# Reading each projection out of PSUM once, with second buffers for keys and queries in the first layer

## The chip, the cores and the metric

The kernel runs on one core of one Trainium2 chip. The metric is the device time of one execution in microseconds (us). The profile is one execution, taken by the hardware profiler on that core. Its engines: TensorE (PE: matrix products and transposes, with its weight loads as PEld), VectorE (DVE), ScalarE (ACT), GpSimd (POOL) and SyncE (SP), whose queue starts most of the DMAs. Matrix products end in PSUM, which has eight banks; one bank holds 128 x 512 floats. Everything else lies in SBUF.

## The reference

One step of a two-layer encoder in float32, with 16 query heads and 4 key/value heads of width 64 and a model width of 1024. There are 1024 tokens of a new stream (8 tiles of 128) and 8 x 16 tokens of running streams with caches (a ninth tile, ST).

```python
# layer 0
qkv = rmsnorm(x, g_norm) @ w_qkv
q = rmsnorm(q.reshape(b, t, N_HEADS, HEAD_DIM), g_q)
k = rmsnorm(k.reshape(b, t, N_KV_HEADS, HEAD_DIM), g_k)
s = q @ k.T * HEAD_DIM ** -0.5 + bias         # own chunk of 64 + 2 before, with sinks
h = h + softmax(s) @ v @ w_o
h = h + square(relu(rmsnorm(h, g) @ w_up)) @ w_down
# layer 1: keys and values by w_kv, queries by w_q_b, own chunk + 8 before,
# learned bias by distance, no sinks; then the same kind of MLP
```

The change lies in what happens between a projection and the normed key or query: each head of 64 values is divided by the root of its mean square.

## The kernel before

**Precision and products.** Each operand is split into a high and a low part (`split`, L106: a copy cast to fp32r, then a subtraction), and each product is made of three matmuls: high by high, high by low, low by high. So a projection of one tile of 128 tokens to 512 columns is 8 x 3 = 24 matmuls of 128 x 512 (`proj`, L182; lines L186 to L188). The MLP has a scheme of its own that saves matmuls; it is not touched.

**Stages.** Per layer: attention, the rest of the output projection with the turning of the residual rows (`wo_phase`), MLP up, MLP down. By the lines at work in the trace, layer 0 runs attention to about 395 us, the handover to the MLP to about 460, up to about 812, down to about 1142. Layer 1 runs attention to about 1640, the handover to about 1690, up to about 2045, down to the end.

**Attention.** For each tile `K1` projects to keys and values (512 columns, 256 each) and `Q1` to queries of half the heads (512 columns). `Q1` runs over all tiles for the first half of the heads and later over all tiles again for the second half; the second time the split hidden rows (tiles hh, hl) come back from DRAM (`R`). When a projection is done, its stage-1 function empties the PSUM bank:

- `kv_stage1` (L237): V is written twice by L245 (ScalarE) and L246 (VectorE), in some tiles once more by L251; the raw keys are copied to kr (L252, ScalarE) and their squares go to kn (L253, ScalarE). kr and kn are the two halves of one tile, kw. Then reduction (L255), scaled mean (L257), power -1/2 on GpSimd (L259), product (L260) and the product with the gain into the tile ks (`k_stack`, L271).
- `q_stage1` (L190): squares to the scratch tile qn (L195, ScalarE), raw queries to the tile qr (L196, ScalarE), then reduction (L198), scaled mean (L203 or L205), power (L207, GpSimd) and product in place (L208).

Later `K2` and `Q2` turn ks and qr on TensorE (`transpose_pairs`, L229) and split the result into KT and qT. Then follow the scores (L349, L400 or L468), their exponentials, the transposes of the probabilities (L293), the products with V (L300, L301) and, half a layer later, the output projection (`WO`, L1474, with matmuls L147 to L149). A `WO` item of kind 0 puts its split input in tiles with the tags ks and kw, kind 1 two of the tag qr, kind 2 hh and hl.

**Buffers.** Tiles of one tag share a fixed number of buffers. A new tile waits until all users of the buffer's last tile are done. In layer 0, kw, ks and qr have one buffer each (2 KB per partition); in layer 1, qr has two. The PSUM role m, which most projections use, has one bank; role s has two in layer 0 and three in layer 1; all else in attention shares the remaining ones (role g).

**Order.** The source gives a program order (for instance three `K1` chunks woven together at the start, then `Q1` and `K2` in turn, then the `plan` of CFG). A planner at compile time turns that into one fixed list for each engine, by priorities and modelled durations (`schedule_with_timeline_sim=True`). On the chip an engine works through its list in order. Any change of buffers or dependencies can therefore also change the lists.

Of the kernel before, what the change touches and what calls it, by code (L numbers as in the profile page):

```python
# [8 lines left out]
F32 = mybir.dt.float32  # L9
F32R = mybir.dt.float32r  # L10
AF = mybir.ActivationFunctionType
# [5 lines left out]
P = 128  # L17
# [6 lines left out]
KV = 4  # L24
G = 4
HD = 64
# [49 lines left out]
class Build:  # L76
# [113 lines left out]
    def q_stage1(self, work, small, ps, t, nb, fold):  # L190
        nc = self.nc
        ps3 = ps.rearrange("p (h d) -> p h d", d=HD)
        qn = self.scratch([P, 8, HD], F32, "qn")
        qr = work.tile([P, 8, HD], F32, tag="qr", name="qr", bufs=self.qrb)
        nc.scalar.activation(qn, ps3, AF.Square)  # L195
        nc.scalar.copy(qr, ps3)  # L196
        ssq = small.tile([P, 8], F32, tag="qssq", name="qssq")
        nc.vector.tensor_reduce(ssq, qn, AX.X, ALU.add)  # L198
        ms = small.tile([P, 8], F32, tag="qms", name="qms")
        e = self.ex[:, t : t + 1]  # L200
        if fold:
            c = C_SL2 + nb * 8
            nc.vector.scalar_tensor_tensor(ms, ssq, e, self.cst[:, c : c + 8], ALU.add, ALU.mult)  # L203
        else:
            nc.vector.tensor_scalar(ms, ssq, e, 1.0 / HD, ALU.add, ALU.mult)  # L205
        rs = small.tile([P, 8], F32, tag="qrs", name="qrs")
        nc.gpsimd.tensor_tensor(rs, ms, self.mhalf[:, 0:8], ALU.pow)  # L207
        self.eng("q").tensor_tensor(qr, qr, rs.unsqueeze(2).to_broadcast([P, 8, HD]), ALU.mult)  # L208
        return qr
# [27 lines left out]
    def kv_stage1(self, work, small, ps, t, gk, gq8, gkq8, vst, v8, kout, vout):  # L237
        nc = self.nc
        ps3 = ps[:, 0:256].rearrange("p (h d) -> p h d", d=HD)
        kw = work.tile([P, 2, KV, HD], F32, tag="kw", name="kw")  # L240
        kr, kn = kw[:, 0], kw[:, 1]
        r = self.rx[:, t : t + 1]
        if vst is not None:
            pv3 = ps[:, 256:512].rearrange("p (h d) -> p h d", d=HD)
            nc.scalar.activation(vst[:, :, 0:HD], pv3, AF.Copy, scale=r)  # L245
            nc.vector.scalar_tensor_tensor(  # L246
                vst[:, :, HD:P], pv3, r, vst[:, :, 0:HD].bitcast(F32), ALU.mult, ALU.subtract
            )
        if vout is not None:
            vsb = v8 if v8 is not None else self.scratch([P, 256], F32, "vsb")  # L250
            nc.scalar.activation(vsb, ps[:, 256:512], AF.Copy, scale=r)  # L251
        nc.scalar.copy(kr, ps3)  # L252
        nc.scalar.activation(kn, ps3, AF.Square)  # L253
        ssq = small.tile([P, KV], F32, tag="kssq", name="kssq")
        nc.vector.tensor_reduce(ssq, kn, AX.X, ALU.add)  # L255
        ms = small.tile([P, KV], F32, tag="kms", name="kms")
        nc.vector.tensor_scalar(ms, ssq, self.ex[:, t : t + 1], 1.0 / HD, ALU.add, ALU.mult)  # L257
        rs = small.tile([P, KV], F32, tag="krs", name="krs")
        nc.gpsimd.tensor_tensor(rs, ms, self.mhalf[:, 0:KV], ALU.pow)  # L259
        nc.vector.tensor_tensor(kn, kr, rs.unsqueeze(2).to_broadcast([P, KV, HD]), ALU.mult)  # L260
        if kout is not None:
            nc.vector.tensor_tensor(kn, kn, gk.unsqueeze(1).to_broadcast([P, KV, HD]), ALU.mult)
            nc.sync.dma_start(kout, kn.rearrange("p h d -> p (h d)"))
        if vout is not None:
            nc.sync.dma_start(vout, vsb)
        return self.k_stack(work, kn, gq8 if kout is not None else gkq8)

    def k_stack(self, work, kn, gq8):
        nc = self.nc
        ks = work.tile([P, KV, HD], F32, tag="ks", name="ks")  # L270
        nc.vector.tensor_tensor(ks, kn, gq8.unsqueeze(1).to_broadcast([P, KV, HD]), ALU.mult)  # L271
        return ks

# [988 lines left out]
    def attention(self, layer):  # L1262
        nc, I = self.nc, self.ins
        A = layer == 0
# [12 lines left out]
        cfg = CFG[layer]  # L1277
        psp = () if A else cfg["psp"]
        self.engs = cfg["eng"]
        with ExitStack() as st:  # L1280
# [6 lines left out]
            work = self.pool(st, f"work{layer}")  # L1287
# [4 lines left out]
            up = self.pool(st, f"unit{layer}")  # L1292
# [6 lines left out]
            if cfg["rx"]:  # L1299
                self.raws += [(ring, "raw2")]  # L1300
            self.qrb = cfg["qrb"]
            self.KT = kvp.tile([P, NT, KV, 2, P], F32R, tag="KT", name="KT")
            self.VS = kvp.tile([P, NT, KV, P], F32R, tag="VS", name="VS")
            v8 = kvp.tile([P, 256], F32, tag="v8", name="v8")
# [169 lines left out]
            def WO(t, half):  # L1474
                o = self.scratch([P, 4, P], F32, "o")
                self.load_halves(layer, half, t, o, second)
                kind = cfg["wt"][t] if half else 0
                if kind == 0:
                    oh = work.tile([P, 4, P], F32R, tag="ks", name="oh")
                    ol = work.tile([P, 4, P], F32R, tag="kw", name="ol")  # L1480
                elif kind == 1:
                    oh = work.tile([P, 4, P], F32R, tag="qr", name="oh", bufs=self.qrb)
                    ol = work.tile([P, 4, P], F32R, tag="qr", name="ol", bufs=self.qrb)
                else:
                    oh = hpool.tile([P, 4, P], F32R, tag="hh", name="oh")
                    ol = hpool.tile([P, 4, P], F32R, tag="hl", name="ol")
                self.split(oh, ol, o, "pool" if "O" in self.engs else "act", "pool" if "o" in self.engs else "dve")
                home = cfg["xt"].get(("AB"[half], t))
                if home == "x":
                    xt = work.tile([P, D], F32, tag="x", name="xo", bufs=2)  # L1490
                elif home in ("hh", "hl"):
                    xt = hpool.tile([P, D], F32, tag=home, name="xo")
                else:
                    xt = self.rawp.tile([P, D], F32, tag="raw", name="xo")
                if home == "keep":
                    self.kept[t] = xt
                nc.sync.dma_start(xt, self.xd[t] if half else x_src(t))
                z = [oh, ol, xt, None]

                def chunk(i):  # L1500
                    n, k = i // 4, i % 4
                    if k == 0:
                        z[3] = self.psum(cfg["wr"][2 * half + n], [P, 512], "ps_mm")
                    ps = z[3]
                    nn = slice(n * 512, n * 512 + 512)
                    self.wo_proj(ps, oh, ol, wo[half], nn, [k])
                    if k == 3:
                        nc.vector.tensor_tensor(xt[:, nn], ps, xt[:, nn], ALU.add)
                        if n == 1:
                            (nc.gpsimd if half else nc.sync).dma_start(self.xd[t], xt)  # L1510

                return [lambda i=i: chunk(i) for i in range(8)]
# [7 lines left out]
            prio = st.enter_context(ExitStack())  # L1520
# [5 lines left out]
            if A:  # L1526
                g = self.load_gains(apool)
# [182 lines left out]
def make_plan(tail):  # L1710
    plan = {}
    for s in range(2 * NT):
# [35 lines left out]

CFG = [
    dict(banks=dict(g=(5, 1), s=(2, 1), m=(1, 1)), q_bufs=4, order={}, plan=make_plan({15: [('A', 0)], 17: [('A', 1)], 19: [('A', 2)], 21: [('A', 3)], 23: [('A', 4)], 25: [('A', 5)], 30: [('A', 6)], 31: [('A', 7)], 32: [('A', 8), ('B', 0), ('B', 4), ('B', 3)]}),  # L1750
        la=3, prio=0, xt={('A', 8): 'x', ('B', 3): 'x', ('B', 0): 'keep', ('B', 4): 'keep'}, late=0, eng='cgu', k2=3, q2=9, lead=3, sf=0, up=(99, 2, 0, 3), ld=((10, 10, 11, 11), (11, 12, 13, 14), (27, 28, 29, 30)), n='g', q='g', qrb=1, np=3, bias_bufs=3, p_bufs=3, psp=(), wr='mmmm', wt=(0, 0, 2, 0, 2, 2, 0, 1, 2), rx=1, kd=1, o2=0, sb=0),
    dict(banks=dict(g=(4, 1), s=(3, 1), m=(1, 1)), q_bufs=4, order={}, plan=make_plan({15: [('A', 0)], 17: [('A', 1)], 19: [('A', 2)], 21: [('A', 3)], 23: [('A', 4)], 25: [('A', 5)], 27: [('A', 8)], 28: [('A', 7)], 29: [('A', 6)], 31: [('B', 0), ('B', 4), ('B', 1)], 32: [('B', 5), ('B', 2), ('B', 3)]}),
        la=2, prio=1000, xt={('B', 0): 'keep', ('B', 4): 'keep', ('B', 1): 'hh', ('B', 5): 'hl', ('B', 2): 'hh', ('B', 3): 'hl'}, late=0, eng='Ogu', k2=3, q2=6, lead=9, sf=0, up=(4, 2, 0, 99), ld=((11, 11, 11, 11), (11, 11, 11, 11), (26, 27, 28, 29)), n='g', q='g', qrb=2, np=2, bias_bufs=2, p_bufs=10, psp=(), wr='mmmm', wt=(0, 0, 0, 1, 1, 1, 1, 1, 2), rx=0, kd=1, o2=1, sb=3),
]

TC_KW = dict(schedule_with_timeline_sim=True)
# [42 lines left out]
```

## Time and profile before

| | |
|---|---|
| median of 3 runs | 2405.27 us (2404.04 to 2407.24) |
| span of the profiled execution | 2399.3 us |
| TensorE busy | 2320.4 us |
| VectorE busy | 1626.3 us |
| ScalarE busy | 1217.9 us |
| mean granted TensorE clock | 0.992 |

The profile gives the span from the first to the last instruction; the execution's own time was not kept, so it is taken as the span and what lies around it: the median is 6.0 us above the span. A row of the timeline is start, length, engine, line, operation, output <- input, shapes, count, and in brackets the engine's idle time just before and what ended it. A row of the waits is who waited for whom: total us, times, longest.

### The profile page before, as it was taken

To read this page: it belongs to the slowest core of one execution; us is meant where nothing else is said; L and a number is where in the kernel's file an instruction comes from. 1 tells how busy PE (TensorE), PEld (TensorE's weight loads), DVE (VectorE), ACT (ScalarE), POOL (GpSimd) and SP (SyncE) were. 2 spreads that over 40 slices of the span, in tenths; PEclk is the share of its full clock that TensorE was granted. 3 is DMA by queue.
4 is the path that set the end of the run, shared out by engine and by line. 5 is a ranking of instruction groups with operands and counts; after the bars stand their busy time and mean duration, and the time that the engine had idled before them with its cause. 6 is when DMAs were issued, how large, how long until landed. Compare 5 with 4: busy or idle time off the path is not lost.

```text
span 2399.3 us, 33421 instructions
## 1 busy us (share of the span) xinstructions
PE 2320.4 (97%) x11621; PEld 1935.5 (81%) x11621; DVE 1626.3 (68%) x3002; ACT 1217.9 (51%) x2423; POOL 535.6 (22%) x828
## 2 busy tenths in 40 slices
PE   7998999899999999999999999998999999999999
PEld 6786877788888888888777788887888888888887
DVE  6687786755655777776567877877655555776674
ACT  4676675555555433232267666665655555333321
POOL 3343332312112100000333434344211211000000
PEclk9998999999999999999999999999999999999999
DMA  7345546244433874342743555555434435744332
GB/s 244 122 127 168 171 156 200 95 155 158 145 128 141 323 245 146 117 141 99 237 149 111 188 161 173 173 169 174 138 127 145 154 137 200 278 140 158 112 116 114
DMA packets 218457, 385.88 MB, mean 161 GB/s; under 512 B 50408, under 2 KB 125104, under 8 KB 211120
## 3 DMA queue, kind: packets, MB, share of 16 engines
q1 hardware_dynamic: 195136, 307.16, 39.0%
q0 software_dynamic: 21776, 71.84, 7.7%
q10 hardware_dynamic: 1376, 4.74, 0.5%
q8 instruction: 92, 1.51, 0.3%
q14 instruction: 77, 0.63, 0.1%
HBM read 246.47 MB, written 136.14 MB: 159 GB/s over the span
## 4 chain that ended last, share of the span: by engine, by line
PE 82%; DMA 7%; DVE 5%; ACT 2%; issue 2%; POOL 1%; SPq 1%; ACTq 0%; DVEq 0%; POOLq 0%
PE ps_x L715 9%; PE ps_x L717 9%; PE ps_x L716 9%; PE ps_y L717 7%; PE ps_y L716 7%; PE ps_y L715 7%; PE ps_mm L186 3%; PE ps_mm L188 3%; PE ps_mm L187 3%; PE ps_tr L293 2%; PE ps_mm L147 2%; PE ps_mm L149 2%; PE ps_mm L148 2%; PE ps_s L717 1%; PE ps_s L716 1%
## 5 line engine op out<-in xcount | busy, mean ns | idle before, releaser
L109 ACT CAST w<-r 128x2048 fp32r<-128x2048 f32 x56 | 107.1, 1913 | 322.9 <-PE ps_y L717 212.1
L715 PE MATMUL ps_x<-w,s 128*128 128x512 f32 x512 | 199.5, 390 | 2.7 <-DVE hc L854 2.1
L717 PE MATMUL ps_x<-w,s 128*128 128x512 f32 x512 | 199.4, 389 | 0.0
L716 PE MATMUL ps_x<-w,s 128*128 128x512 f32 x512 | 199.2, 389 | 0.0
L186 PE MATMUL ps_mm<-w,hh 128*128 128x512 f32 x432 | 175.0, 407 | 13.8 <-ACT kw L253 5.1
L188 PE MATMUL ps_mm<-w,hl 128*128 128x512 f32 x432 | 174.3, 403 | 1.7 <-DMA hl<-hTd 1.4
L187 PE MATMUL ps_mm<-w,hh 128*128 128x512 f32 x432 | 172.5, 400 | 0.7 <-DVE w L159 0.7
L109 ACT CAST s<-s 128x2048 fp32r<-128x2048 f32 x56 | 107.1, 1913 | 117.9 <-DMA s<-hd 108.6
L115 DVE TENSOR_TENSOR w<-r,w 128x2048 fp32r<-128x2048 f32 x56 | 128.2, 2290 | 51.9 <-ACT w L109 51.9
L715 PE MATMUL ps_x<-sx,w 128*128 128x512 f32 (+1 forms) x408 | 157.8, 387 | 4.6 <-ACT hc L834 2.7
L1021 DVE TENSOR_TENSOR x<-ps_y,x 128x512 f32<-128x512 f32 x136 | 92.3, 687 | 101.1 <-PE ps_y L717 101.0
L717 PE MATMUL ps_x<-sx,w 128*128 128x512 f32 (+1 forms) x408 | 154.1, 378 | 0.0
L716 PE MATMUL ps_x<-sx,w 128*128 128x512 f32 (+1 forms) x408 | 154.1, 378 | 0.0
L109 ACT CAST w<-ru 128x512 fp32r<-128x512 f32 (+1 forms) x160 | 110.0, 708 | 85.3 <-PE ps_y L716 32.0
L717 PE MATMUL ps_y<-w,s 128*128 128x512 f32 x384 | 149.5, 389 | 0.0
L716 PE MATMUL ps_y<-w,s 128*128 128x512 f32 x384 | 149.4, 389 | 0.0
L715 PE MATMUL ps_y<-w,s 128*128 128x512 f32 x384 | 149.4, 389 | 0.0
L115 DVE TENSOR_TENSOR s<-s 128x2048 fp32r<-128x2048 f32 x56 | 128.1, 2287 | 26.5 <-ACT s L109 26.5
L115 DVE TENSOR_TENSOR ptl<-ps_tr,pth 128x512 fp32r<-128x512 f32 x180 | 122.6, 685 | 24.8 <-ACT pth L109 19.0
L115 DVE TENSOR_TENSOR w<-ru,w 128x512 fp32r<-128x512 f32 (+1 forms) x160 | 126.6, 793 | 10.9 <-ACT w L109 10.8
L109 ACT CAST pth<-ps_tr 128x512 fp32r<-128x512 f32 x180 | 104.8, 594 | 47.9 <-PE ps_tr L293 39.3
L115 DVE TENSOR_TENSOR wq<-ru,wq 128x1024 fp32r<-128x1024 f32 x32 | 39.7, 1240 | 131.9 <-ACT wq L109 131.9
(280 smaller groups left out, 6573.3 us busy)
## 6 DMA issues: line engine op xcount, KB each, us to landing
s<-hd SPq DMA_DIRECT2D x56, 1024.0 KB, 4.7
ru<-in_w_up SPq DMA_DIRECT2D x64, 512.0 KB, 3.9
r<-in_w_down SPq DMA_DIRECT2D x32, 1024.0 KB, 5.7
hd<-hc POOLq DMA_DIRECT2D x128, 256.0 KB, 2.7
hd<-hs POOLq DMA_DIRECT2D x96, 256.0 KB, 2.5
x<-xd SPq DMA_DIRECT2D x41, 512.0 KB, 4.6
o<-oTd SPq DMA_DIRECT2D x52, 256.0 KB, 4.1
hTd<-hh SPq DMA_DIRECT2D x36, 256.0 KB, 4.5
```

The costliest lines, as they stand in the source:

```text
L109: a = nc.scalar.copy(hi, src)
L115: return a, e.tensor_tensor(lo, src, hi.bitcast(F32), ALU.subtract)
L147: nc.tensor.matmul(ps, oh[:, k, :], w[:, 0, k, nn], start=(k == 0), stop=False)
L148: nc.tensor.matmul(ps, oh[:, k, :], w[:, 1, k, nn], start=False, stop=False)
L149: nc.tensor.matmul(ps, ol[:, k, :], w[:, 0, k, nn], start=False, stop=(k == 3))
L186: nc.tensor.matmul(ps, a, w[:, 0, k, :], start=(k == 0), stop=False)
L187: nc.tensor.matmul(ps, a, w[:, 1, k, :], start=False, stop=False)
L188: nc.tensor.matmul(ps, b, w[:, 0, k, :], start=False, stop=(k == KC - 1))
L715: a = mm(ps, ah, bh, start=first, stop=False, skip_group_check=True)
L716: mm(ps, ah, bl, start=False, stop=False, skip_group_check=True)
L717: return a, mm(ps, al, bh, start=False, stop=last, skip_group_check=True)
L1021: tt(xs[t][:, N[n]], ps, xs[t][:, N[n]], ALU.add)
```

## The change

In both stage-1 functions the raw projection is copied out of PSUM first, and the square then reads the copy in SBUF. The tags kw and ks get a number of buffers from the configuration (`krb`), 2 in layer 0 and 1 in layer 1; `WO` names the same number for its kind 0. In the first entry of CFG `qrb` goes from 1 to 2; in the second it stays at 2. Nothing else in CFG changes.

```diff
         qn = self.scratch([P, 8, HD], F32, "qn")
         qr = work.tile([P, 8, HD], F32, tag="qr", name="qr", bufs=self.qrb)
-        nc.scalar.activation(qn, ps3, AF.Square)
         nc.scalar.copy(qr, ps3)
+        nc.scalar.activation(qn, qr, AF.Square)
...
-        kw = work.tile([P, 2, KV, HD], F32, tag="kw", name="kw")
+        kw = work.tile([P, 2, KV, HD], F32, tag="kw", name="kw", bufs=self.krb)
...
         nc.scalar.copy(kr, ps3)
-        nc.scalar.activation(kn, ps3, AF.Square)
+        nc.scalar.activation(kn, kr, AF.Square)
...
-        ks = work.tile([P, KV, HD], F32, tag="ks", name="ks")
+        ks = work.tile([P, KV, HD], F32, tag="ks", name="ks", bufs=self.krb)
...
             self.qrb = cfg["qrb"]
+            self.krb = cfg["krb"]
...
-                    oh = work.tile([P, 4, P], F32R, tag="ks", name="oh")
-                    ol = work.tile([P, 4, P], F32R, tag="kw", name="ol")
+                    oh = work.tile([P, 4, P], F32R, tag="ks", name="oh", bufs=self.krb)
+                    ol = work.tile([P, 4, P], F32R, tag="kw", name="ol", bufs=self.krb)
```

More of the change, by code (lines that the diff above doesn't have):

```diff
@@ L1750 @@
     dict(banks=dict(g=(5, 1), s=(2, 1), m=(1, 1)), q_bufs=4, order={}, plan=make_plan({15: [('A', 0)], 17: [('A', 1)], 19: [('A', 2)], 21: [('A', 3)], 23: [('A', 4)], 25: [('A', 5)], 30: [('A', 6)], 31: [('A', 7)], 32: [('A', 8), ('B', 0), ('B', 4), ('B', 3)]}),
-        la=3, prio=0, xt={('A', 8): 'x', ('B', 3): 'x', ('B', 0): 'keep', ('B', 4): 'keep'}, late=0, eng='cgu', k2=3, q2=9, lead=3, sf=0, up=(99, 2, 0, 3), ld=((10, 10, 11, 11), (11, 12, 13, 14), (27, 28, 29, 30)), n='g', q='g', qrb=1, np=3, bias_bufs=3, p_bufs=3, psp=(), wr='mmmm', wt=(0, 0, 2, 0, 2, 2, 0, 1, 2), rx=1, kd=1, o2=0, sb=0),
+        la=3, prio=0, xt={('A', 8): 'x', ('B', 3): 'x', ('B', 0): 'keep', ('B', 4): 'keep'}, late=0, eng='cgu', k2=3, q2=9, lead=3, sf=0, up=(99, 2, 0, 3), ld=((10, 10, 11, 11), (11, 12, 13, 14), (27, 28, 29, 30)), n='g', q='g', qrb=2, krb=2, np=3, bias_bufs=3, p_bufs=3, psp=(), wr='mmmm', wt=(0, 0, 2, 0, 2, 2, 0, 1, 2), rx=1, kd=1, o2=0, sb=0),
     dict(banks=dict(g=(4, 1), s=(3, 1), m=(1, 1)), q_bufs=4, order={}, plan=make_plan({15: [('A', 0)], 17: [('A', 1)], 19: [('A', 2)], 21: [('A', 3)], 23: [('A', 4)], 25: [('A', 5)], 27: [('A', 8)], 28: [('A', 7)], 29: [('A', 6)], 31: [('B', 0), ('B', 4), ('B', 1)], 32: [('B', 5), ('B', 2), ('B', 3)]}),
-        la=2, prio=1000, xt={('B', 0): 'keep', ('B', 4): 'keep', ('B', 1): 'hh', ('B', 5): 'hl', ('B', 2): 'hh', ('B', 3): 'hl'}, late=0, eng='Ogu', k2=3, q2=6, lead=9, sf=0, up=(4, 2, 0, 99), ld=((11, 11, 11, 11), (11, 11, 11, 11), (26, 27, 28, 29)), n='g', q='g', qrb=2, np=2, bias_bufs=2, p_bufs=10, psp=(), wr='mmmm', wt=(0, 0, 0, 1, 1, 1, 1, 1, 2), rx=0, kd=1, o2=1, sb=3),
+        la=2, prio=1000, xt={('B', 0): 'keep', ('B', 4): 'keep', ('B', 1): 'hh', ('B', 5): 'hl', ('B', 2): 'hh', ('B', 3): 'hl'}, late=0, eng='Ogu', k2=3, q2=6, lead=9, sf=0, up=(4, 2, 0, 99), ld=((11, 11, 11, 11), (11, 11, 11, 11), (26, 27, 28, 29)), n='g', q='g', qrb=2, krb=1, np=2, bias_bufs=2, p_bufs=10, psp=(), wr='mmmm', wt=(0, 0, 0, 1, 1, 1, 1, 1, 2), rx=0, kd=1, o2=1, sb=3),
 ]
```

## The prediction

> **What bounds the kernel now.** I read the page's busy table and chain first, then busy time by stage, then TensorE's waits, then those waits one by one in the timeline.
>
> ```profile
> span 2399.3 us, 33421 instructions
> PE 2320.4 (97%) x11621; PEld 1935.5 (81%) x11621; DVE 1626.3 (68%) x3002; ACT 1217.9 (51%) x2423; POOL 535.6 (22%) x828
> PE 82%; DMA 7%; DVE 5%; ACT 2%; issue 2%; POOL 1%; SPq 1%; ACTq 0%; DVEq 0%; POOLq 0%
> ...
> 0.00:395.00 395.00, 362.20 (x1906) 0.97 0.51 167
> 395.00:460.00 65.00, 57.66 (x324) 1.00 0.46 155
> 460.00:812.00 352.00, 351.85 (x1805) 1.00 0.44 155
> 812.00:1142.00 330.00, 328.48 (x1447) 1.00 0.47 165
> 1142.00:1640.00 498.00, 476.18 (x2561) 1.00 0.55 171
> ```
>
> TensorE is busy for 97% of the span and makes 82% of the chain: the kernel ends when TensorE has done its list. A row of the stage table is window, length, PE busy, granted clock, DMA share, GB/s. The edited functions run only in the two attention stages (0 to 395 and 1142 to 1640 us). There TensorE idles 395.00 - 362.20 = 32.8 us and 498.00 - 476.18 = 21.8 us. The matmuls stay as they are, so the change can only take from, or add to, these 54.6 us and the stretches of low clock that follow some gaps. The MLP (460 to 1142) has almost no idle to lose.
>
> Which of the idle is the change's? TensorE's waits, as total, times, longest:
>
> ```profile
> PE ps_n L662 <- DVE sx L115: 9.4, 10, 2.4
> PE ps_mm L186 <- ACT kw L253: 5.1, 3, 4.0
> PE ps_mm L186 <- ACT qr L196: 2.5, 3, 1.0
> PE ps_q L229 <- DVE qT L115: 1.9, 1, 1.9
> PE ps_q L229 <- DVE qr L208: 0.3, 1, 0.3
> ```
>
> A projection (L186) waits for ScalarE's last read of the bank that it is to write: 5.1 us behind L253, 2.5 us behind L196. So 7.6 us is a ceiling on what the earlier release can take away directly.
>
> **Part 1: one read of PSUM instead of two.** Removed from the bank's hold is the second read. In the K/V step copy L252 comes first, then square L253; in the query step square L195 first, then copy L196.
>
> ```profile
> 39.65 0.60 ACT L195 ACTIVATE qn<-ps_mm 128x512 f32<-128x512 f32 x1 [2.05 <-PE ps_mm L188]
> 40.15 0.58 ACT L196 COPY qr<-ps_mm 128x512 f32<-128x512 f32 x1
> 64.23 0.37 ACT L252 COPY kw<-ps_mm 128x256 f32<-128x256 f32 x1 [0.65 <-DVE VS L246]
> 64.50 0.39 ACT L253 ACTIVATE kw<-ps_mm 128x256 f32<-128x256 f32 x1
> ...
> 32.48 0.77 PE L186 MATMUL ps_mm<-w,hh 128*128 128x512 f32 x1 [4.01 <-ACT kw L253]
> 64.94 0.49 PE L186 MATMUL ps_mm<-w,hh 128*128 128x512 f32 x1 [0.69 <-ACT kw L253]
> 75.35 0.50 PE L186 MATMUL ps_mm<-w,hh 128*128 128x512 f32 x1 [0.97 <-ACT qr L196]
> 219.73 0.51 PE L186 MATMUL ps_mm<-w,hh 128*128 128x512 f32 x1 [0.49 <-ACT qr L196]
> 1229.84 0.50 PE L186 MATMUL ps_mm<-w,hh 128*128 128x512 f32 x1 [1.05 <-ACT qr L196]
> 1341.98 0.50 PE L186 MATMUL ps_mm<-w,hh 128*128 128x512 f32 x1 [0.40 <-ACT kw L253]
> ```
>
> Keys: the bank was free at 64.50 + 0.39 = 64.89, and will be at 64.23 + 0.37 = 64.60: 0.29 us earlier. Queries: free at 40.15 + 0.58 = 40.73, and will be at 39.65 + 0.58 = 40.23: 0.50 us earlier. Six TensorE gaps end on these releases, three of each kind: 3 x 0.29 + 2 x 0.50 + 0.49 (that gap has no more) = 2.4 us. Bounds: at least nothing, if something else of the same instant comes next; at most 7.6 us. I take **-2.4**, since each gap ends within 0.1 us of the read. ScalarE is 51% busy and not the limit.
>
> **Part 2: the square comes later.** It now needs the copy's result. A dependent pair of the same size, from the MLP, shows what that costs:
>
> ```profile
> 485.18 0.63 ACT L788 ACTIVATE hc<-hc 128x512 f32<-128x512 f32 x1 [1.41 <-DVE hc L836]
> 485.84 0.63 ACT L789 ACTIVATE hc<-hc 128x512 f32<-128x512 f32 x1
> ```
>
> There the second starts 0.66 us after the first, 0.03 us after its end. So copy 0.58, then 0.03, then square 0.63: the square is ready 1.24 us after the start, where it was ready after 0.60: **0.64 us later** for a query tile, with reduction, power and scaling behind it. For a key tile, copy and square at half size (0.37 + 0.03, then about 0.42 by the same ratio) give 0.82 against 0.27 + 0.39 = 0.66: 0.16 later. A delay counts only where TensorE stands before the transposes of that tile. "PE ps_q L229 <- DVE qr L208: 0.3, 1, 0.3" says that this happens once in 36 query tiles. The price is one exposure, **+0.6**; from nothing, if the order moves, up to four exposures, 2.6.
>
> The Trainium skill, "ScalarE: Activation LUTs", section "What ACT_TABLE_LOAD costs", says that back-to-back ACTIVATEs overlap by about 93 ns. The independent pair above agrees (0.60 - 0.50 = 0.10 us) and the dependent pair does not (no overlap). With the overlap the delay would be about 0.55 instead of 0.64, and the sum the same to 0.1 us.
>
> **Part 3: second buffers in layer 0.** With one buffer, the copy of the next tile waits for the previous tile's last reader.
>
> ```profile
> 36.94 0.37 ACT L252 COPY kw<-ps_mm 128x256 f32<-128x256 f32 x1 [4.20 <-DVE ks L271]
> 49.41 0.59 ACT L196 COPY qr<-ps_mm 128x512 f32<-128x512 f32 x1 [3.46 <-PE ps_q L229]
> 50.10 0.69 DVE L208 TENSOR_TENSOR qr<-qr,qrs 128x512 f32<-128x512 f32 x1
> 53.80 0.69 DVE L115 TENSOR_TENSOR qT<-ps_q,qT 64x512 fp32r<-64x512 f32 x1 [0.26 <-ACT qT L109]
> 54.63 0.63 PE L229 MATMUL ps_q<-identr,qr 128*128 128x128 f32 x4 [1.94 <-DVE qT L115]
> 56.17 0.80 PE L188 MATMUL ps_mm<-w,hl 128*128 128x512 f32 x1 [0.22 <-DVE hl L115]
> 55.00:60.00 5.00, 4.78 (x17) 0.66 0.69 228
> ```
>
> These are ScalarE's stalls while layer 0 starts, when three key and three query tiles follow each other closely: 4.20 us for kw, 3.46 us for qr. Both go. TensorE feels them late: its next real gap is 1.94 us at 54.63, with 0.22 us at 56.17, and after it the clock is granted at 0.66 for 4.78 busy us, which costs (1 - 0.66) x 4.78 = 1.6 us. Together 3.8 us. What is late next: the transposes at 54.63 waited for a PSUM bank (freed by L115 at 53.80 + 0.69 = 54.49), not for qr, which was ready at 50.79. So the gap goes only if those transposes, or the reads in front of that L115, move forward with the earlier data. The bounds are 0 and -3.8. I take **-3.8**: the whole startup list of ScalarE and VectorE moves up by some of those 4 us, more than the 1.94 us gap.
>
> Whether the low clock goes with the gap is a matter of its own. The Trainium skill, "TensorE: Matmul & The Clock Gate", section "Part 1: The HAM clock gate", says that the clock halves after one idle window of about 3.4 us, and "Part 4: PE-mode transpose" that transposes do not count as work. By that rule the stretch from 51.4 (last projection) to 55.3 us (next one), with transposes and few scores in it, is idle enough, and a shorter one would keep the clock; the 0.66 agrees. If only the gap went and not the low clock, the part would be worth 2.2 instead of 3.8.
>
> The same buffers take the output projection's split tiles in layer 0. TensorE has no gap before L147 there, so this is worth nothing. The 6 KB per partition (three tiles of 2 KB) shift what lies behind them, and so what the handover to the MLP is laid over; its 7.3 us of idle (65.00 - 57.66) wait mainly for VectorE (9.4 us at L662 over both layers), not for memory. I price it at 0. In layer 1, where qr has two buffers already, a copy that waits for its slot now holds up its square too, which used to run ahead. The worst such tile:
>
> ```profile
> 1399.79 0.58 ACT L196 COPY qr<-ps_mm 128x512 f32<-128x512 f32 x1
> 1417.28 0.27 PE L229 MATMUL ps_q<-identr,qr 128*128 128x128 f32 x1
> ```
>
> From its copy to its transposes lie 17.5 us, several times what square, reduction, power and scaling take. Nothing.
>
> **Sum.** -2.4 + 0.6 - 3.8 = -5.6 us on the profiled span, 2393.7. The median, 2405.27, is 6.0 us above the span; with that left as it is: **2399.7 us**, 0.23% faster. About 0.2% (4.8 us) is what a measurement of this kernel can tell from no change.
>
> **The rivals.** (a) *The buffers are hidden anyway*: the gap at 54.63 is a matter of PSUM banks and stays. Then 2405.3 - 2.4 + 0.6 = **2403.5**, no change. For it: the releaser named is L115. Against it: all in front of that L115 gets its data earlier.
>
> (b) *A newly planned order blocks an engine at a start: slower.* Each engine runs a list that is fixed at compile time from modelled durations; earlier readiness makes other lists. The present list shows what a bad place costs:
>
> ```profile
> 29.46 1.83 DVE L159 SCALAR_TENSOR_TENSOR w<-raw,gcol,w 128x512 fp32r<-128x512 f32 x2 [3.06 <-POOL w L156]
> 31.72 0.37 ACT L252 COPY kw<-ps_mm 128x256 f32<-128x256 f32 x1 [3.35 <-DVE VS L246]
> 32.50:35.20 2.70, 2.70 (x7) 0.50 1.04 388
> ```
>
> VectorE stands 3.06 us before a weight split whose data is late (DMA at full share), with the V split L246 behind it; ScalarE's copy waits 3.35 us for that, TensorE 4.01 us for the bank, and then runs at clock 0.50 for 2.70 us, 1.35 us lost. One such place costs 4.0 + 1.4 = 5.4 us. One more eats the whole gain (2405.1); from the second on it is slower: 2399.7 + 10.8 = **2410.5**. It can happen only where weights stream in, at the start of each attention stage, which speaks against two.
>
> (c) *More goes than I count.* In 178 to 222 us queries are reloaded for the second head half, and there too copies wait for the single qr slot:
>
> ```profile
> 182.73 0.77 PE L186 MATMUL ps_mm<-w,hh 128*128 128x512 f32 x1 [1.95 <-DMA hh<-hTd]
> 183.00:189.00 6.00, 6.00 (x14) 0.50 0.96 318
> 202.11 0.47 PE L186 MATMUL ps_mm<-w,hh 128*128 128x512 f32 x1 [2.38 <-DMA hh<-hTd]
> ```
>
> If the freed bank lets the projections be spread so that these loads are covered, 1.95 + 2.38 us and the slow 6 us (half of it, 3.0) go as well: 2399.7 - 7.3 = **2392.4**. Against it: the loads wait for the buffer of the hidden rows, which the change does not touch.
>
> That the change does not do what it says has no place here: the copy frees the bank by the code itself.
>
> **How the numbers follow.** Forecast 2399.7: 0.42. Rival (a) 2403.5: 0.30. Rival (b) 2410.5: 0.17. Rival (c) 2392.4: 0.11. Below 2400.5 is faster: most of the forecast (0.38 of 0.42) with (c), 0.49; within 0.2% is (a) and the rest of the forecast, 0.34; above 2410.1 is (b), 0.17. The range goes from 2391 (past (c), with a little of the release's ceiling) to 2411 (just past (b)). The cases other than (b) alone would give 2391 to 2405.
>
> **What would show it.** Right: the rows "ps_mm L186 <- ACT kw L253" and "<- ACT qr" gone or half as long; no wait of L252 for L271 nor of L196 for L229 near 36 to 50 us; the gap at 54 us and the low clock after it gone; square starts 0.6 us after copy. Wrong: the first stage's idle of 32.8 us unchanged (rival a), a new gap over 3 us with clock 0.5 behind it in the first 60 us of a stage (rival b), waits for hh below 1 us around 180 to 205 us (rival c), or a changed MLP span, which none of this explains.

## The result and the profile after

The change makes the kernel **slower by 0.35%**: 2412.48 us median (2407.14 to 2418.82, 12 runs) against 2404.65 us (2397.10 to 2410.63, 12 runs), ratio 1.0035, 95% interval 1.0022 to 1.0047. By the medians that is 7.8 us more where 5.6 us less was forecast, and 1.5 us past the upper end of the range.

The page of the changed kernel, its stage table (window, length, TensorE busy, granted clock, DMA share, GB/s) and TensorE's waits:

```profile
span 2405.7 us, 33285 instructions
...
PE 2325.5 (97%) x11621; PEld 1940.2 (81%) x11621; DVE 1626.4 (68%) x3002; ACT 1219.7 (51%) x2423; POOL 539.0 (22%) x828
```

```profile
0.00:395.00 395.00, 360.76 (x1914) 0.97 0.52 168
395.00:460.00 65.00, 58.79 (x324) 0.97 0.44 152
...
1142.00:1640.00 498.00, 476.12 (x2534) 0.98 0.55 169
...
1370.00:1375.00 5.00, 5.00 (x14) 0.50 0.18 46
```

```profile
PE ps_mm L186 <- DMA hh<-hTd: 8.1, 4, 5.3
...
PE ps_s L349 <- DVE qT L115: 5.7, 2, 5.3
PE ps_s L349 <- ACT p L364: 4.9, 4, 1.3
PE ps_s L349 <- DMA KT<-KT: 4.8, 1, 4.8
```

Engines do the same work, and the idle of the first stage is no smaller: 395.00 - 360.76 = 34.2 us, before 32.8. But it is other idle. The waits for kw and qr that the forecast wanted gone are gone or short, and in the rows above stand 8.1 + 5.7 + 4.9 + 4.8 = 23.5 us of waits, of which the kernel before has the 4.3 us for hh (1.95 + 2.38 in the forecast's rows) and hardly any of the rest.

These waits took the place of others: over the whole span TensorE idles 2405.7 - 2325.5 = 80.2 us, and before 2399.3 - 2320.4 = 78.9. What grew is its busy time, by 5.1 us for the same 11621 matmuls, at a mean granted clock of 0.989 against 0.992. In the attention stage of layer 1 the idle is that of before (21.9 us against 21.8) and the clock is 0.98 against 1.00. So in this pair of profiles the net loss is low clock more than idle: the last row above is the stretch behind the gap at 1370 us, at clock 0.50. The timeline shows where (start, length, engine, line, operation; in brackets the idle before it and what ended it):

```profile
31.01 0.47 PE L186 MATMUL ps_mm<-w,hh 128*128 128x512 f32 x1 [1.64 <-ACT kw L252]
50.82 0.66 PE L229 MATMUL ps_q<-identr,qr 128*128 128x128 f32 x4 [0.78 <-DVE qT L115]
...
168.80 0.98 PE L349 MATMUL ps_s<-KT,qT 128*128 128x256 f32 x3 [4.76 <-DMA KT<-KT]
...
275.93 0.50 PE L349 MATMUL ps_s<-KT,qT 128*128 128x256 f32 x2 [1.34 <-ACT p L364]
...
337.77 1.53 PE L349 MATMUL ps_s<-KT,qT 128*128 128x256 f32 x4 [5.33 <-DVE qT L115]
...
1370.00 0.77 PE L186 MATMUL ps_mm<-w,hh 128*128 128x512 f32 x1 [5.34 <-DMA hh<-hTd]
```

The start goes as forecast: the gap near 54 us is now 0.78 us long (was 1.94) and no low clock follows it. Then come three long gaps that the kernel before does not have at these places, and a series of four short ones like that at 275.93. None of them is at the start of a stage. The longest one in layer 0, on ScalarE and VectorE:

```profile
330.41 0.59 ACT L195 COPY qr<-ps_mm 128x512 f32<-128x512 f32 x1 [0.73 <-PE ps_mm L188]
330.89 2.94 ACT L109 CAST w<-raw 128x1024 fp32r<-128x1024 f32 x3
333.73 0.63 ACT L196 ACTIVATE qn<-qr 128x512 f32<-128x512 f32 x1
334.26 0.56 ACT L109 CAST qT<-ps_q 64x512 fp32r<-64x512 f32 x1
```

```profile
332.54 1.22 DVE L115 TENSOR_TENSOR w<-raw,w 128x1024 fp32r<-128x1024 f32 x1
...
333.81 1.22 DVE L115 TENSOR_TENSOR w<-raw,w 128x1024 fp32r<-128x1024 f32 x1
...
335.02 1.22 DVE L115 TENSOR_TENSOR w<-raw,w 128x1024 fp32r<-128x1024 f32 x1
...
336.94 0.69 DVE L115 TENSOR_TENSOR qT<-ps_q,qT 64x512 fp32r<-64x512 f32 x1
```

TensorE stands from 332.4 to 337.8 us before a product with qT. The split that makes qT stands in both lists behind three weight splits (2.94 us on ScalarE, 3 x 1.22 on VectorE). No data is late here. It is the order of the lists, and that order is the compile-time planner's, which made new lists for the changed kernel. At 168.80 it is the same kind: the split of KT stands behind weight splits on VectorE. At 1370.00 the product waits for the reload of hh, which stands behind three other transfers on SP, and TensorE's list has too little other work in front of it. The three transfers explain little of the gap: the first of them starts at 1360.07 us and the reload at 1361.89, 8.1 us ahead of the product. Two rows of SP's queue:

```profile
1361.39 0.41 SPq L1498 DMA_DIRECT2D xo<-xd  x1
1361.89 0.38 SPq L1359 DMA_DIRECT2D hh<-hTd  x1
```

**Theory A**: the planner's new lists lose the time. **Theory B**: the change itself loses it, through the square that now depends on the copy. **Theory C**: the buffers lose it, through the 6 KB that they take.

### The profile page after: what moved, and what is told of

The parts are those of the page before. It is cut to its first block, busy times and chain, and to the rows that moved or that the text cites. A ratio compares the mean times of both kernels' runs of the same rounds, so it can differ in the third digit from the quotient of the medians.

```text
span 2405.7 us, 33285 instructions
## 1 busy us (share of the span) xinstructions
PE 2325.5 (97%) x11621; PEld 1940.2 (81%) x11621; DVE 1626.4 (68%) x3002; ACT 1219.7 (51%) x2423; POOL 539.0 (22%) x828
## 4 chain that ended last, share of the span: by engine, by line
PE 80%; DMA 7%; DVE 6%; ACT 4%; issue 2%; POOL 1%; SPq 1%; ACTq 0%; DVEq 0%; POOLq 0%
PE ps_x L715 9%; PE ps_x L717 9%; PE ps_x L716 9%; PE ps_y L717 7%; PE ps_y L716 7%; PE ps_y L715 7%; PE ps_mm L186 3%; PE ps_mm L188 3%; PE ps_mm L187 3%; PE ps_tr L293 2%; PE ps_s L717 1%; PE ps_s L716 1%; PE ps_s L715 1%; PE ps_z L717 1%; PE ps_z L716 1%
## 5 line engine op out<-in xcount | busy, mean ns | idle before, releaser
L115 DVE TENSOR_TENSOR w<-r,w 128x2048 fp32r<-128x2048 f32 x56 | 128.3, 2291 | 53.0 <-ACT w L109 53.0
L115 DVE TENSOR_TENSOR s<-s 128x2048 fp32r<-128x2048 f32 x56 | 128.1, 2287 | 25.1 <-ACT s L109 25.1
L115 DVE TENSOR_TENSOR ptl<-ps_tr,pth 128x512 fp32r<-128x512 f32 x180 | 122.9, 686 | 20.4 <-ACT pth L109 18.7
L115 DVE TENSOR_TENSOR w<-ru,w 128x512 fp32r<-128x512 f32 (+1 forms) x160 | 126.6, 793 | 11.1 <-ACT w L109 11.0
L115 DVE TENSOR_TENSOR wq<-ru,wq 128x1024 fp32r<-128x1024 f32 x32 | 39.7, 1240 | 132.2 <-ACT wq L109 132.2
```

The lines of the kernel that those rows point to most:

```text
L115: return a, e.tensor_tensor(lo, src, hi.bitcast(F32), ALU.subtract)
```

## The experiments

Each was timed in five rounds beside the kernel before. Where a list is held, the order of every engine in the two attention stages is written into the kernel as data and put on the planner as an order without a wait:

```diff
+def pin(nc, tc):
...
+        for a, b in zip(o, o[1:]):
+            tc.add_manual_dep(e[int(b)], e[int(a)].name, AFTER, reason="order")
...
         Build(tc, ins, outs).run()
+        pin(nc, tc)
```

What the holding itself costs was not timed, since no run holds a kernel's own lists. The profiles show no added work: buffers_only_old_order, with its lists held, has 33411 instructions, and the kernel before 33421.

The added lines shift the line numbers: in some rows below the scores are L353 instead of L349, the transposes of queries L233 or L237 instead of L229, and so on.

| kernel | reads of PSUM | second buffers | lists | ratio to before, 95% interval |
|---|---|---|---|---|
| the change | one | yes | new | 1.0035 (1.0022 to 1.0047) |
| old_reads_new_order | two | yes | new | 1.0035 (1.0022 to 1.0048) |
| new_reads_old_order | one | yes | old | 1.0009 (0.9995 to 1.0024) |
| buffers_only_old_order | two | yes | old | 1.0038 (1.0024 to 1.0053) |
| reads_only_old_order | one | no | old | 1.0035 (1.0021 to 1.0049) |
| memory_only | two | no, but their memory | old | 1.0022 (1.0009 to 1.0036) |
| layer0_only | one in layer 0 | yes | new in layer 0 | 1.0018 (1.0007 to 1.0030) |
| layer1_only | one in layer 1 | no | a third list in layer 1 | 1.0075 (1.0057 to 1.0093) |
| layer1_new_order | one in layer 1 | no | new in layer 1 | 1.0022 (1.0010 to 1.0034) |
| new_order_mended | one | yes | new, three places moved | 1.0022 (1.0009 to 1.0036) |
| early_new_then_old | one in layer 0 | yes | new to 120 us, then old | 0.9976 (0.9964 to 0.9988) |
| cut_120_again | the same kernel | | | 0.9960 (0.9949 to 0.9972) |
| early_new_old_reads | two | yes | new to 120 us, then old | 0.9995 (0.9983 to 1.0006) |
| early_new_reads_both | one | yes | new to 120 us, then old | 0.9987 (0.9976 to 0.9998) |
| cut_205 | one in layer 0 | yes | new to 205 us, then old | 0.9977 (0.9967 to 0.9987) |
| cut_300 | one in layer 0 | yes | new to 300 us, then old | 1.0020 (1.0007 to 1.0032) |
| cut_345 | one in layer 0 | yes | new to 345 us, then old | 1.0042 (1.0029 to 1.0055) |

0.1% is 2.4 us. "Old" and "new" lists are those of the kernel before and of the changed one. In new_reads_old_order and early_new_reads_both two query tiles of layer 1 keep the two reads, in reads_only_old_order seven query tiles do.

### Reads against order

new_reads_old_order has the reads and the buffers of the change and the lists of before; each copy and its square change places within their pair.

> The changed kernel (one read of PSUM, second buffers in layer 0), but with every engine's list in both attention stages held in the order that it had before the change; each copy and its square change places within their pair. Two query tiles of layer 1, whose copy waits for its slot, keep the old form. Theory A (the loss comes from the new lists that the compile-time planner makes): the gains come without the new gaps, 2405 - 2 to 2405 - 6, about 2400. Theory B (the loss comes from the square that now depends on the copy and runs later, whatever the order): the loss of 7 to 8 us stays, about 2412.

old_reads_new_order is the other half of the crossing:

```diff
-        nc.scalar.copy(qr, ps3)
-        nc.scalar.activation(qn, qr, AF.Square)
+        nc.scalar.activation(qn, ps3, AF.Square)
+        nc.scalar.copy(qr, ps3)
...
-        nc.scalar.activation(kn, kr, AF.Square)
+        nc.scalar.activation(kn, ps3, AF.Square)
```

> The other half of the crossing: the buffers and every engine's list of the changed kernel in both attention stages, but square and copy both read PSUM again, the square directly ahead of (query) or behind (key) its copy. Theory A (new lists): the new gaps are there again, 2410 to 2414. Theory B (dependent square): without the dependence the loss is gone, about 2405. If the squares set far behind their copies are what the new lists lose by, then between the two, since here they stand beside the copies.

Measured: 1.0009 and 1.0035. With the new lists the whole loss is there without any dependent square, and with squares beside their copies. Theory B falls as the cause of the loss, and so does the thought that squares set far behind their copies cost it. It does not follow that the lists alone make it. The fourth cell of the crossing is buffers_only_old_order, told further below, with two reads and the old lists: 1.0038. With two reads the loss is there under either list, and only with one read does it depend on the list (1.0035 against 1.0009, intervals that just touch). So the crossing by itself does not prove theory A. What proves it for layer 0 are the cuts below. The timeline of old_reads_new_order has the same gaps at the same places:

```profile
169.35 0.98 PE L349 MATMUL ps_s<-KT,qT 128*128 128x256 f32 x3 [4.94 <-DMA KT<-KT]
...
337.87 1.48 PE L349 MATMUL ps_s<-KT,qT 128*128 128x256 f32 x4 [5.32 <-DVE qT L115]
...
1371.94 0.77 PE L186 MATMUL ps_mm<-w,hh 128*128 128x512 f32 x1 [5.14 <-DMA hh<-hTd]
```

With one read and the old lists the loss is gone, as A says, but the gain of 2 to 6 us that A promised did not come either. One reason stands in the timeline of new_reads_old_order: the gap near 54 us stays.

```profile
55.13 0.63 PE L237 MATMUL ps_q<-identr,qr 128*128 128x128 f32 x4 [2.54 <-DVE qT L118]
```

### Layer by layer

layer0_only and layer1_only choose the reads by layer and leave the planner free:

```diff
+        if self.rd:
+            nc.scalar.copy(qr, ps3)
+            nc.scalar.activation(qn, qr, AF.Square)
+        else:
+            nc.scalar.activation(qn, ps3, AF.Square)
+            nc.scalar.copy(qr, ps3)
...
+            self.rd = A
```

(layer1_only has `self.rd = not A`, and one buffer of each tag in layer 0.)

> The whole change in layer 0 alone, layer 1 with the two reads of PSUM as before; the planner is left free (its lists in layer 0 come out as in the changed kernel, in layer 1 as before). From the two traces, layer 0 gains about 6 us early, gives it back by its end, and reaches the MLP 0.5 us later: 2405 to 2406 by theory A and by the trace. If the loss is spread over both layers in equal parts (theory B, 18 query tiles in each): about 2409.

> The single read of PSUM in layer 1 alone, layer 0 as before; the planner is left free, and its lists in layer 1 are neither those of before nor those of the changed kernel. If the reads themselves lose in layer 1 (theory B): about 2411 to 2412. Theory A: any value that a third list may give, 2403 to 2415; the place of the new gaps would then not be that of the changed kernel (none at the reload of the hidden rows behind 1370 us).

Measured: 1.0018 and 1.0075. Layer 0 loses more than the two profiles had shown (the MLP's first product, ps_x, starts at 440.44 us in the changed kernel and at 442.00 in the one before); what they hid is told in the last section. layer1_only lies 18 us above before, outside what either theory named: the planner's third list for layer 1 is far worse than its second. So layer 1 was run again with the lists of the changed kernel held:

> Layer 0 as before, lists and all; in layer 1 the single read and the lists of the changed kernel. If the loss of 8 us is the sum of the layers (layer 0 alone measured 4 more than before): about 4 more, 2407 to 2408. If the changed kernel's layer 1 loses only because of how layer 0 leaves it: as before, 2403.

Measured: 1.0022. The layers add up, 0.18 + 0.22 = 0.40% against 0.35%, well within the intervals. And the same edit to layer 1 costs 0.22% or 0.75%, by the list that it happens to get. That is an effect of the list alone. How much of the 0.22% is the list's and how much the single read's stays open: no run has two reads with the new lists in layer 1 alone. Nor is its gap at the reload always the same: 5.34 us in the changed kernel, 2.63 here.

### Where the new lists lose

In new_order_mended three places of the new lists are moved by hand: the three weight splits of 331 us behind the query split, the key split of 164 us ahead of weight splits, the reload at 1361 us ahead of three transfers.

> The changed kernel and its lists, with three places mended by hand: near 331 us the three weight casts (ScalarE) and the three weight splits (VectorE) go behind the query split that TensorE waits for; near 164 us the key split goes ahead of five weight splits on VectorE and its copy ahead of two weight loads on SP; near 1361 us the reload of the hidden rows goes ahead of three other transfers on SP. If the loss is these places of the new lists: 5.3 - 1 at the first gap, about 3 of the 4.8 at the second, about 1 of the 5.3 at the third, so 8 us less than the changed kernel's 2412, about 2404. If the lists lose in many small places instead, or the time goes on to the next wait: 2409 to 2412.

Measured: 1.0022 against 1.0035 for the lists unmended, about 3 us better with intervals that overlap, so a gain of the three moves is not shown. The gap at 1370 is gone. The other two turned into the next wait, as the timeline of new_order_mended shows:

```profile
174.70 0.50 PE L349 MATMUL ps_s<-KT,qT 128*128 128x256 f32 x2 [3.02 <-DVE qT L115]
...
345.07 0.79 PE L349 MATMUL ps_s<-KT,qT 128*128 128x256 f32 x2 [4.93 <-ACT p L364]
```

```profile
341.03 2.94 ACT L109 CAST w<-raw 128x1024 fp32r<-128x1024 f32 x3
```

qT is on time at 345 us, and now the exponentials stand behind the same three weight casts on ScalarE. There is not one blocked instruction. That the lists hold too little for TensorE there while weights are split, whatever their order, is a reading and was not tried.

The next kernels keep the change in layer 0 and the old reads and lists in layer 1. In layer 0 the new lists run up to some time, and what is left follows in the order of before.

> The change in layer 0 alone; there the lists of the changed kernel up to 120 us, where TensorE is ahead of before, then what is left in the order of before; layer 1 and its lists as before. If the early gain (26.98 + 33.99 + 49.36 against 24.49 + 32.15 + 45.15 busy us, 8.5 us) lasts when the later lists are the old ones: 2397 to 2400. If the next waits, on transfers that do not move (hidden rows and weights at 170 to 205 us), take the lead back whatever the list: about 2404.

> The same kernel as early_new_then_old. If its gain is real: 0.9964 to 0.9988 of before again, about 2395 to 2398. If that comparison was luck: about 1.000.

> As early_new_then_old, with the new lists of layer 0 kept up to 205 us. From the traces, 160 to 200 us holds 30.09 busy us with the new lists and 29.69 with the old ones behind the cut, so the gaps at 168 and 197 us take the place of old ones: as the cut at 120 us, 0.997 to 0.999 of before. If the key split's place at 164 us is what loses: 4 to 5 us more than the cut at 120 us, 1.000.

> New lists up to 300 us. From the traces, 232 to 300 us holds 63.12 busy us with the new lists and 68.00 with the old ones: about 5 us more than the cut at 205 us, 0.999 to 1.001 of before. If the loss lies only in the weight splits near 331 us: as the cut at 205 us.

> New lists up to 345 us. From the traces, 300 to 345 us holds 38.33 busy us at clock 0.92 with the new lists and 41.93 at 0.96 with the old ones, 5 us of work: about 5 us more than the cut at 300 us, 1.001 to 1.003 of before, as layer 0 with new lists throughout (1.0018). If the later order mends it: as the cut at 300 us.

Measured, by the cut: 120 us **0.9960** (and 0.9976 the first time), 205 us 0.9977, 300 us 1.0020, 345 us 1.0042; new lists through the whole of layer 0 (layer0_only) 1.0018. All of these have the same reads and buffers, and differ in the order alone. This settles theory A for layer 0: the first 120 us of the new lists gain, and what follows loses more than that. From 120 to 205 us no loss is shown (the same kernel gave 0.9960 and 0.9976, and cut_205 is 0.9977): the gap at KT takes the place of an old gap. From 205 to 300 us the kernel loses most, 0.43% or 10 us, and to 345 us another 0.22% or 5 us. The stage tables of cut_205, cut_300 and cut_345, in this order:

```profile
232.00:300.00 68.00, 68.00 (x382) 1.00 0.55 180
300.00:345.00 45.00, 42.12 (x232) 0.96 0.46 140
```

```profile
232.00:300.00 68.00, 63.00 (x340) 1.00 0.51 164
300.00:345.00 45.00, 41.56 (x230) 0.96 0.39 122
```

```profile
232.00:300.00 68.00, 63.47 (x352) 1.00 0.53 164
300.00:345.00 45.00, 38.16 (x205) 0.96 0.39 127
```

TensorE falls from full to 63 of 68 us where the new list goes on past 232 us, in gaps of 0.8 to 1.3 us before L349 that wait for an exponential and before L574, and by 3.4 more where it goes on past 300. These 5 us are half of what the runs lose between 205 and 300 us. The other half is not found in one stretch and stays open. cut_345 is slower than layer0_only, which the expectation did not say: the old order behind a late cut does not fit. So what a later cut loses is not all the doing of the stretch that was added; the old order that takes over has a part in it, and the two were not separated.

The kernel cut at 120 us is faster than the kernel before, by 0.24% and 0.40% in the two comparisons (5.8 and 9.6 us).

### Reads, buffers and memory by themselves

> The second buffers in layer 0 alone, two reads of PSUM as before, lists in both attention stages as before. By the forecast's third part: 3.8 us less, 2399.5. If the gap near 54 us can only go with another list (new reads and buffers in the old order kept a gap of 2.5 us there): as before, 2403 +- 1.

> The single read of PSUM alone, in both layers, without the second buffers and with the lists of before (seven query tiles whose copy waits for its slot keep the old form). By the forecast's parts 1 and 2: 2.4 - 0.6 = 1.8 us less than before. From the runs so far (buffers alone +0.38%, buffers with reads +0.09%, same lists): the reads are worth 0.29%, 7 us, so 2394. If the reads are worth nothing by themselves: as before, 2401.

> Before, with the three tiles of layer 0 twice as wide (half of each unused): the memory of the second buffers (6 KB) without the buffers. Every list in the attention stages is that of before; the order at the handover to layer 0's MLP becomes that of the kernels with buffers. If the 9 us that the buffers alone cost come from the memory and the handover it leads to (the forecast priced this shift at 0): about 2409 to 2410. If they come from the buffers' use (which tile goes where, which wait moves): as before, 2401; what lies between shows a part of each.

memory_only widens the tiles instead of doubling them:

```diff
+    def wide(self, work, tag, name, dt, shape, bufs):
...
+        f = work.tile([P, 1024 if self.wd else 512], dt, tag=tag, name=name, bufs=bufs)
...
-        qr = work.tile([P, 8, HD], F32, tag="qr", name="qr", bufs=self.qrb)
+        qr = self.wide(work, "qr", "qr", F32, [P, 8, HD], self.qrb)
```

Measured, all with the old lists in attention: buffers alone 1.0038, reads alone 1.0035, memory alone 1.0022, reads and buffers together 1.0009. None of the four gains, and the two halves of the change cost more apart than together. buffers_only_old_order (5 runs) loses as much as the changed kernel, without its new lists: theory C, taken as the buffers and all that they bring, is not excluded by it.

A part of the memory's price is at the handover to the MLP. The planner's order there changes as soon as the tiles are larger. TensorE's waits from 430 to 470 us and a row of the stage table of memory_only, and then the same of before:

```profile
PE ps_n L669 <- DVE sx L115: 5.2, 6, 2.2
PE ps_x L722 <- ACT hc L841: 1.3, 1, 1.3
PE ps_x L722 <- ACT hc L846: 0.5, 1, 0.5
...
440.00:460.00 20.00, 13.93 (x82) 0.83 0.38 133
```

```profile
PE ps_n L662 <- DVE sx L115: 3.2, 5, 1.6
PE ps_x L715 <- ACT hc L839: 1.4, 1, 1.4
PE ps_x L715 <- ACT hc L834: 1.4, 1, 1.4
PE ps_z L715 <- ACT w L109: 1.0, 1, 1.0
PE ps_z L717 <- DVE w L115: 0.4, 1, 0.4
...
440.00:460.00 20.00, 12.66 (x90) 1.00 0.33 111
```

The waits for sx grow by 2.0 us, those for hc and w shrink from 4.2 to 1.8, and the clock costs (1.00 - 0.83) x 13.93 = 2.4 us: 2.0 us in all. So theory C holds a part: 0.22%, 5 us by the runs (2 to 9). 2 us of it are seen at the handover, and where the rest lies stays open, as does the rest of what the buffers alone lose. The handover's list is another one in every kernel with the buffers, the fastest too. In the changed kernel it is again another than in memory_only, so the 5 us need not be its price there.

Reads alone lose at the start, where there is only one buffer for queries. ScalarE's and TensorE's rows of reads_only_old_order:

```profile
49.17 0.59 ACT L203 COPY qr<-ps_mm 128x512 f32<-128x512 f32 x1 [5.57 <-PE ps_q L237]
49.79 0.63 ACT L204 ACTIVATE qn<-qr 128x512 f32<-128x512 f32 x1
```

```profile
54.82 0.42 PE L357 MATMUL ps_s<-KT,qT 128*128 128x128 f32 x2 [1.72 <-DVE qT L118]
57.11 1.09 PE L237 MATMUL ps_q<-identr,qr 128*128 128x128 f32 x4 [1.86 <-DVE qT L118]
```

The copy waits for its slot, and the square, which used to run ahead of that wait, now stands behind the copy. One gap of 1.94 us became two, 3.58 us. With the second buffer (new_reads_old_order) that copy starts at 45.24 us, as soon as its projection is done, so here the reads need the buffers.

### What the early gain is made of

> As early_new_then_old (0.24% faster than before), with two reads of PSUM again: buffers, and the early part of the new lists alone. If the early gain is that of the second buffers and of the lists which they allow: 2395 to 2397. If the single read brings it: 2405 to 2410, as with the buffers alone.

> As early_new_then_old, with the single read in layer 1 as well (lists of before there, two tiles in the old form). If the single read is worth something under the old lists (up to 7 us over both layers): 2391 to 2394. If it is worth nothing in layer 1, where only 1.5 us of gaps end on such a read: as early_new_then_old, 2395.

Measured: 0.9995 with two reads, against 0.9976 and 0.9960 with one in layer 0: the single read is worth 0.2 to 0.35%, 5 to 8 us, where the buffers and the early lists are given (the intervals overlap in the first comparison and are apart in the second). With one read in layer 1 too, 0.9987: no further gain, rather a loss, which the first comparison alone (0.9976) would not tell from none. In all of these the gap near 54 us is short, 0.78 to 1.15 us, as in this row of cut_120_again:

```profile
54.03 0.66 PE L233 MATMUL ps_q<-identr,qr 128*128 128x128 f32 x4 [0.78 <-DVE qT L115]
```

The low clock behind it is gone in cut_120_again (1.00 from 55 to 60 us), but not in the profile of early_new_old_reads, whose gap is the one of 1.15 us:

```profile
55.00:60.00 5.00, 4.67 (x14) 0.66 0.90 235
```

## Why the prediction was wrong

**The step that failed** is rival (b)'s place and chance: "It can happen only where weights stream in, at the start of each attention stage, which speaks against two." The forecast saw that earlier readiness makes other lists, then let the new lists bring their gain for nothing and looked for harm only at the starts. A row of the kernel before spoke against that, a gap in the middle of the stage that ends on a weight split:

```profile
178.53 0.33 PE L574 MATMUL ps_utp<-identr,sp 128*128 128x128 f32 x1 [3.23 <-DVE w L159]
```

What the runs showed in its place: in layer 0, with reads and buffers the same, the new lists gain 0.24 to 0.40% when they are kept to 120 us and lose 0.18% when they are kept throughout. So 10 to 14 us are lost behind 120 us, most of it behind 205, and none of it at a start. Layer 1 adds 0.22%, of which the list's share is open; its longest gap lies at a reload 230 us into the stage. Weights are split in the middle of the stage too (near 164 and 331 us), so a weight split can stand in front of something urgent there.

The price of one bad place, 5.4 us, was made of a gap of 4.0 and low clock of 1.4. The three gaps are 4.76, 5.33 and 5.34 us long, and with the low clock behind it the third alone costs 5.34 + (1.00 - 0.50) x 5.00 = 7.8 us. Behind the other two the clock is 0.50 as well (170 to 175 and 335 to 340 us). So there were three places instead of two, each dearer, while other idle went. That the rival's time, 2410.5 us, is near the 2412.5 measured is therefore partly luck; its place and its chance, 0.17, were wrong.

**The sum of the gains, 5.6 us**, was near. early_new_then_old, which has the gains of layer 0 without the later lists, gained 5.8 and 9.6 us, the memory's cost already in it. The terms do not agree one by one, so this too is partly luck.

- *Part 1 (-2.4)*: right in sign under two of the lists. In layer 0 the single read is worth 5 to 8 us beside buffers and early lists, and under the old lists 1.0038 against 1.0009, 7 us. That is more than forecast, with intervals that touch or overlap in two of the three comparisons. Under the changed kernel's own lists it is worth nothing (1.0035 with one read and with two), without the buffers it lost (1.0035), and in layer 1 it brought nothing.
- *Part 2 (+0.6)*: not the cause. Without any dependent square the loss is the same, under the new lists. That a square behind a waiting copy stalls was priced at nothing for layer 1; where one buffer made it bite, in reads_only_old_order, it cost about 1.6 us of gaps and more of low clock.
- *Part 3 (-3.8)*: right in mechanism, and with the condition that the forecast named: the gap "goes only if those transposes, or the reads in front of that L115, move forward". With the old lists it stayed (1.94 us with buffers alone, 2.54 with the reads), with the new ones it shrank to 0.78 in the changed kernel, and the low clock went. Its size is not shown by itself: early_new_old_reads has the shorter gap without the single read, with the low clock still there in its profile and the memory's cost in it, and is at 0.9995. What this part gains belongs to the same new lists whose rest lost more.
- *The 6 KB (0)*: mis-sized. 0.22%, about 5 us, by memory_only with its own list at the handover. The handover's order moves when the tiles grow.
- *Rival (a)* held for the kernel with the old lists: 1.0009, no change.
- *Rival (c)*: not seen. In layer 0 the waits for hh fell from 4.3 to 2.8 us, not below 1; of the 8.1 us in the whole span 5.3 are the new gap in layer 1.

## What to carry to other kernels

When a planner orders the engines' lists from modelled durations, a change of buffers or dependencies is two changes, the one written and a new order, and the second can be the larger. Cross the two, by holding the old order with the new code and the new order with the old code, before the change itself is judged, and fill all four cells: here three of them lose alike, and two cells alone would have given the whole loss to the lists. Holding the order also paid: the change in layer 0, with the new lists kept only where they are ahead, turned a loss of 0.18% into a gain of 0.24 to 0.40%. None of the kernels that kept the old lists throughout attention came out faster than the kernel before.

## What the runs showed of the hardware

The first long gap of the program, TensorE's wait near 32 us while weights stream in, varies from execution to execution with the same lists. The row of before has 4.01 us, and the changed kernel's profile 1.64, which reads like a gain. But cut_300 and cut_205 share the new lists to 205 us (two rows, one of each):

```profile
31.47 0.47 PE L186 MATMUL ps_mm<-w,hh 128*128 128x512 f32 x1 [1.41 <-ACT kw L256]
```

```profile
33.81 0.47 PE L186 MATMUL ps_mm<-w,hh 128*128 128x512 f32 x1 [4.29 <-ACT kw L256]
```

and layer1_new_order, which has the old lists in layer 0, shows 1.71 us there:

```profile
31.10 0.47 PE L186 MATMUL ps_mm<-w,hh 128*128 128x512 f32 x1 [1.71 <-ACT kw L257]
```

So this gap differs by 3 us from one profile to the next with the same lists, and such a difference between two single profiles is no evidence here. It also hid what layer 0 lost in the changed kernel's profile: layer0_only has the same lists in layer 0, and its row shows 4.54 us.

```profile
32.81 0.77 PE L186 MATMUL ps_mm<-w,hh 128*128 128x512 f32 x1 [4.54 <-ACT kw L256]
```

Short gaps spread over a long stretch left the clock alone: in cut_300 the stretch 232 to 300 us has 5 us of idle in pieces of up to 1.34 us, and the granted clock is 1.00 throughout. The Trainium skill, "TensorE: Matmul & The Clock Gate", section "Part 1: The HAM clock gate", lets the clock halve only after an idle window of about 3.4 us, and this row agrees. The length of a gap does not tell it alone. In the kernel before, the gap of 1.94 us at 54.63 us, with transposes around it, is followed by a clock of 0.66, and one of 1.92 us at 93.99 us is not followed by a lower clock. No run here separates what makes the difference.
